# A hybrid attention and DeltaNet layer: the scan's small products grouped over both directions, the decay tile in two passes, softmax sums broadcast by transposes

## The chip, the cores and the metric

The kernel runs on one core of one Trainium2 chip. The metric is the device time of one execution in microseconds (us). Before the change three runs gave 896.90, 898.29 and 898.93 us; their median, 898.29 us, is the time to compare with.

## The reference, cut to what matters

One layer over 512 latent tokens and 256 context tokens, width 1024. A combined projection feeds two mixers: windowed attention with a softmax, and a gated DeltaNet that is scanned over chunks of 64 tokens, forwards and backwards, with 8 heads of 64. The scan's step, for each head and direction, is

```python
def step(S, xs):
    w_c, uv_c, qd_c, intra_c, kt_c, gl_c = xs
    u = uv_c - jnp.einsum('bhck,bhkv->bhcv', w_c, S)
    o = jnp.einsum('bhck,bhkv->bhcv', qd_c, S) + jnp.einsum('bhij,bhjv->bhiv', intra_c, u)
    S = jnp.exp(gl_c)[..., None, None] * S + jnp.einsum('bhck,bhcv->bhkv', kt_c, u)
    return S, o
```

The decays and rates of the scan come from 32 columns of the projection, `da` (through a softplus) and `db` (through a sigmoid). Attention outputs are divided by the softmax sums. After both mixers come their projections, gates, an output projection and a squared-ReLU MLP.

## The kernel before

**Engines and precision.** All data are float32. A projection is three TensorE matmuls per 128x128 block of weights (`mm3`, lines 312 to 314): both operands are split into a rounded high part and a low rest, and high times high, high times low and low times high are added up in one accumulator (in the profile `wh` and `wl` are the parts of a weight tile, `m` is any tile of the big arena). Other matmuls run on plain float32 and take two records each in the trace. PSUM's eight banks are handed out by `bank()`.

**Order of the work.** `tile_layer` records all instructions; then `arrange` lists them anew. `listed` walks through time with a table of costs: each engine takes the ready instruction that was recorded first, and TensorE stays with whole-array or with small-tile matmuls while the other kind is at most `STICK` = 50 instructions older. It also reckons with the arrival of TensorE's instructions, in blocks of 256 (`asked`). The order that results is fixed for each engine.

**The stages, in the order of the profile.**
- 0 to 60 us: modulation (`ada`, `columns`, `features`), with three early projection tiles. The first of these is `T_AB`: 32 useful columns (`da`, `db`) in a 128-wide block, the rest zeros. Its accumulator goes through lines 716 to 726 (a softplus and a sigmoid on 16 partitions each) into `gb`, which the small matmuls of line 753 read.
- To 280 us: key, query and value tiles, the matrices of the scan's chunks (`chunk_mats`), their inversion by a chain of pairs of VectorE operations (`invert`, lines 883 and 884), and attention (`scores`, `outputs`). Line 632 transposes the probabilities by `PE.transpose`; line 653 spreads a column of reciprocal softmax sums over 128 partitions by a plain float32 matmul with the identity, four for each of the eight (block, kv) units, and line 654 multiplies by them.
- 288 to 456 us: the scan, 4 context steps and 8 latent steps, each for two directions (`chain_step`), woven with filler matmuls (`br_a` at line 1105, `gate_tiles` at line 1059) and with `combine` (lines 904 to 915, 32x32 products).
- From 456 us: norm of the scan's output (line 1355, transposes at 1360), the branch and output projections and the MLP. `late_mod` (line 1124) is VectorE work that is spread over the scan and what follows.

**One scan step.** For a direction `d` and its state `S` a step has 64x64 products on TensorE: k times S and, for latent chunks, q times S (line 1175, 8 + 8 matmuls), then VectorE forms R (1179, 1180); XA times R gives u (1194, 8 matmuls); VectorE forms uk (1200), ScalarE copies u to `us` (1204) and, four times, the q product scaled to `zq` (1206); K times uk (1214, 8 matmuls) and VectorE's subtraction (1225) give the new state; IA times us (1232, 8 matmuls) and the additions of lines 1237 to 1242 give the output. All products of a direction lie in its own two banks, `zb[d]`. The 64x64 products are "small": TensorE goes from whole-array matmuls to them and back. A **visit** in this text is an uninterrupted run of small matmuls in TensorE's order.

## Time and profile before

| what | value |
|---|---|
| median of the three runs | 898.29 us |
| the profiled execution's own time | 895.83 us |
| its span in the profile | 894.1 us |
| mean granted TensorE clock | 0.998 |
| TensorE busy | 868.7 us of the span |
| VectorE, ScalarE busy | 652.3 us, 496.5 us |
| TensorE visits, counted in the order | 78, of which 45 in the latent scan |

PE is TensorE's matmul pipeline, PEld its weight loads, DVE VectorE, ACT ScalarE, SP the engine that issues most DMAs. A row of the timeline has the start in us, the duration in us, the engine, the line, the operation, `output<-input`, the shape and the number of records; `[0.63 <-PE ...]` is idle time before the row and what ended it. Matmuls overlap, so what one costs is the distance from its start to the next start.

### The profile page before, as it was taken

Reading aid. Unit: us, or ns where it says so; the run is one execution under the profiler, and the core shown is the slowest. Engines: PE = TensorE matmul, PEld = TensorE weight load, DVE = VectorE, ACT = ScalarE, POOL = GpSimd, SP = SyncE. Lnnn points to the kernel's source line nnn. Section 1 sums busy time; section 2 is a strip of 40 time slices with the busy share of each in tenths; the row PEclk is TensorE's granted clock in tenths of the full one; section 3 lists DMA queues with packets and bytes.
Section 4 is the critical chain, followed back from the end, with each engine's and each line's share of the span. In section 5 each row is a group of like instructions: output and inputs, shape, how many; then the busy total and the mean of one; then the engine's idle time right before and its main releaser. Section 6 shows DMA issues by size and latency. Waiting matters only on the chain.

```text
span 894.1 us, 18035 instructions
## 1 busy us (share of the span) xinstructions
PE 868.7 (97%) x7564; PEld 719.3 (80%) x7564; DVE 652.3 (73%) x1111; ACT 496.5 (56%) x881; POOL 26.1 (3%) x42
## 2 busy tenths in 40 slices
PE   7999999999999999999999999999999999999998
PEld 6778778877777777767678899888998899889886
DVE  5756899986778999856687878993868377638641
ACT  5549874486668886676654435561554245425520
POOL 0000001010000001100000000000000000000000
PEclk9999999999999999999999999999999999999999
DMA  9834455433111136623144653633314341332031
GB/s 354 325 101 95 91 129 124 108 78 66 36 36 32 64 115 244 211 73 97 49 154 154 226 175 118 209 121 128 108 48 138 98 137 52 118 114 100 1 118 47
DMA packets 31985, 107.13 MB, mean 120 GB/s; under 512 B 4000, under 2 KB 4512, under 8 KB 31904
## 3 DMA queue, kind: packets, MB, share of 16 engines
q1 hardware_dynamic: 29600, 97.59, 31.9%
q0 software_dynamic: 2304, 8.39, 5.7%
q8 instruction: 59, 0.97, 0.4%
q14 instruction: 22, 0.18, 0.1%
HBM read 103.87 MB, written 2.10 MB: 119 GB/s over the span
## 4 chain that ended last, share of the span: by engine, by line
PE 49%; DVE 3%; ACT 2%; DMA 1%; issue 1%; DVEq 0%; SPq 0%; ACTq 0%
PE banks L1528 12%; PE banks L313 10%; PE banks L314 10%; PE banks L312 10%; PE banks L1059 5%; DMA m<-in_wm 1%; DVE m L221 1%; PE banks L1175 1%; DVE m L318 1%; ACT m L220 1%; DVE m L320 1%; DMA m<-in_wada 0%; PE banks L1232 0%; PE banks L1214 0%; PE banks L1194 0%
## 5 line engine op out<-in xcount | busy, mean ns | idle before, releaser
L312 PE MATMUL banks<-m,wh 128*128 128x512 f32 (+1 forms) x568 | 213.0, 375 | 0.0
L313 PE MATMUL banks<-m,wh 128*128 128x512 f32 (+1 forms) x568 | 210.3, 370 | 0.6 <-DVE m L221 0.6
L314 PE MATMUL banks<-m,wl 128*128 128x512 f32 (+1 forms) x568 | 210.2, 370 | 0.0
L290 ACT ACTIVATE wh<-wr 128x1024 fp32r<-128x1024 f32 (+1 forms) x92 | 90.5, 984 | 135.5 <-PE banks L313 95.6
L1528 PE MATMUL banks<-m,m 128*128 128x256 f32 x1008 | 123.3, 284 | 3.6 <-ACT m L220 3.1
L1528 PEld LDWEIGHTS banks<-m,m 128*128 128x128 f32 x1008 | 122.0, 192 | 5.1 <-ACT m L220 3.7
L220 ACT ACTIVATE m<-m 128x512 fp32r<-128x512 f32 (+2 forms) x118 | 81.8, 719 | 75.3 <-PE banks L1528 16.0
L314 PEld LDWEIGHTS banks<-m,wl 128*128 128x128 f32 x568 | 106.9, 188 | 18.9 <-issue 0.7
L313 PEld LDWEIGHTS banks<-m,wh 128*128 128x128 f32 x568 | 107.0, 188 | 18.5 <-DVE m L221 1.1
L312 PEld LDWEIGHTS banks<-m,wh 128*128 128x128 f32 x568 | 107.1, 189 | 18.3 <-issue 0.5
L1059 PE MATMUL banks<-m,wh 128*128 128x512 f32 x320 | 108.0, 408 | 1.7 <-ACT m L181 0.8
L221 DVE TENSOR_TENSOR m<-m,m 128x512 fp32r<-128x512 f32 (+2 forms) x118 | 92.4, 805 | 21.4 <-ACT m L220 14.7
L295 DVE TENSOR_TENSOR wl<-wr,wh 128x1024 fp32r<-128x1024 f32 (+1 forms) x76 | 84.2, 1110 | 16.4 <-ACT wh L290 14.2
L1655 DVE SCALAR_TENSOR_TENSOR m<-banks,modT,m 128x512 f32<-128x512 f32 x32 | 24.0, 750 | 74.8 <-PE banks L314 74.7
L1059 PEld LDWEIGHTS banks<-m,wh 128*128 128x128 f32 x320 | 58.2, 188 | 14.5 <-ACT m L181 1.4
L1059 PE MATMUL banks<-m,wl 128*128 128x512 f32 x160 | 64.6, 404 | 0.6 <-DVE wl L295 0.6
L313 PE MATMUL banks<-m,m 128*128 128x256 f32 (+1 forms) x136 | 45.7, 342 | 0.5 <-DVE m L320 0.5
L312 PE MATMUL banks<-m,m 128*128 128x256 f32 (+1 forms) x136 | 45.0, 345 | 0.9 <-ACT m L319 0.8
L314 PE MATMUL banks<-m,m 128*128 128x256 f32 (+1 forms) x136 | 44.5, 336 | 0.2 <-DVE m L295 0.2
L1124 DVE SCALAR_TENSOR_TENSOR m<-m,m 128x1024 f32<-128x1024 f32 x32 | 38.7, 1219 | 5.0 <-DMA m<-in_wada 5.0
L1059 PEld LDWEIGHTS banks<-m,wl 128*128 128x128 f32 x160 | 30.0, 188 | 7.3 <-DVE wl L295 1.0
L181 ACT ACTIVATE m<-banks,st 128x512 f32<-128x512 f32 (+1 forms) x32 | 23.5, 738 | 20.3 <-DVE st L589 20.1
(258 smaller groups left out, 1345.4 us busy)
## 6 DMA issues: line engine op xcount, KB each, us to landing
m<-in_wada SPq DMA_DIRECT2D x48, 512.0 KB, 5.7
wr<-in_wm SPq DMA_DIRECT2D x40, 512.0 KB, 3.6
wr<-in_win SPq DMA_DIRECT2D x39, 512.0 KB, 3.5
m<-in_wm SPq DMA_DIRECT2D x24, 512.0 KB, 3.6
wl<-in_win POOLq DMA_DIRECT2D x16, 512.0 KB, 5.5
m<-in_xT SPq DMA_DIRECT2D x8, 512.0 KB, 5.5
wr<-in_wbr SPq DMA_DIRECT2D x16, 256.0 KB, 2.6
wr<-in_wout SPq DMA_DIRECT2D x8, 512.0 KB, 3.9
```

The costliest lines, as they stand in the source:

```text
L181: r = A.activation(out_, in_, func, **kw)
L220: A.activation(r32(hi), src, AF.Copy)
L221: (eng or V).tensor_tensor(r32(lo), src, hi, op=ALU.subtract)
L290: upper[0] = A.activation(r32(hi), raw, AF.Copy)
L295: V.tensor_tensor(r32(lo), raw, hi, op=ALU.subtract)
L312: PE.matmul(acc, w[0][:, k, :], xhi, start=(start and i == 0), stop=False)
L313: PE.matmul(acc, w[0][:, k, :], xlo, start=False, stop=False)
L314: r = PE.matmul(acc, w[1][:, k, :], xhi, start=False, stop=(stop and i == n - 1))
L1059: PE.matmul(acc.ap, w[x][:, k, :], hx[k][y], start=(k == p == 0), stop=(k == KT - 1 and p == 2))
L1124: V.scalar_tensor_tensor(wa.ap, wa.ap, 0.5, scr.ap, op0=ALU.mult, op1=ALU.mult, accum_out=modT[:, grp, j:j + 1])
L1528: PE.matmul(dst, r32(self.w[w][i][:, k * P:(k + 1) * P]), xs7[x][k][j], start=(n == 0), stop=(n == 11))
L1655: V.scalar_tensor_tensor(xn_[ct], accs[ct].ap, modT[:, 3, ct:ct + 1], xn_[ct], op0=ALU.mult, op1=ALU.add)
```

## The change

**The decay tile.** `T_AB` leaves the packed weights; its 64 columns come as an own array `wab`. Their high parts fill columns 0 to 63 of one 128-wide tile and their low parts columns 64 to 127 (`wload_ab`), so two matmuls per block instead of three give all products, and rows 64 to 127 of the accumulator are added to rows 0 to 63 afterwards: a ScalarE copy and a VectorE addition stand ahead of the softplus. The load is 256 KB instead of 512 KB.

**Softmax sums.** Line 653's matmul becomes `PE.transpose`, 32 in all.

**The scan.** The matmuls of a step are put in three lists for both directions (`runs`): list 0 k times S, list 1 XA times R, list 2 K times uk, q times S (moved here from list 0) and IA times us. `listed` holds all matmuls of such a list back until the last of them is ready and then releases them together. q times S and IA times us get two banks of their own, `qo`, shared by the directions; the scaled copies to `zq` come after list 2. From the start of the latent scan fillers have two banks instead of four.

**The planner's model of instruction arrival** has other constants. `LIMIT` is so large that its branch is never taken.

```diff
+    def wload_ab():
+        raw = wp.tile([P, KT, P], F32, tag="wr", bufs=NWR, name=nm("wr"))[:, :4].rearrange("p k (h c) -> p (k h) c", h=2)
+        nc.sync.dma_start(out=raw, in_=I["wab"])
+        b = alloc(1024)
+        ebufs.append(b)
+        w = b.ap.rearrange("p (k c) -> p k c", k=KT)
+        upper[0] = A.activation(r32(w[:, :, :CH]), raw, AF.Copy)
+        V.tensor_tensor(r32(w[:, :, CH:]), raw, w[:, :, :CH], op=ALU.subtract)
+        return r32(w), None
...
             PE.matmul(acc, w[0][:, k, :], xhi, start=(start and i == 0), stop=False)
-            PE.matmul(acc, w[0][:, k, :], xlo, start=False, stop=False)
-            r = PE.matmul(acc, w[1][:, k, :], xhi, start=False, stop=(stop and i == n - 1))
+            end = stop and i == n - 1
+            r = PE.matmul(acc, w[0][:, k, :], xlo, start=False, stop=(end and w[1] is None))
+            if w[1] is not None:
+                r = PE.matmul(acc, w[1][:, k, :], xhi, start=False, stop=end)
...
-            PE.matmul(rb[:, j * P:(j + 1) * P], st[:, 2, j:j + 1].broadcast_to([P, P]), ident, start=True, stop=True)
+            PE.transpose(rb[:, j * P:(j + 1) * P], st[:, 2, j:j + 1].broadcast_to([P, P]), ident)
...
-    V.tensor_scalar(ad, acc[0:16, :TOK], dtb[0:16], None, op0=ALU.add)
+    ab = t2[64:128]
+    A.activation(t2[0:64], acc[64:128, :TOK], AF.Copy)
+    V.tensor_tensor(ab, t2[0:64], acc[0:64, :TOK], op=ALU.add)
+    acc.free()
+    V.tensor_scalar(ad, ab[0:16], dtb[64:80], None, op0=ALU.add)
...
+        def small_product(n, out_, w, x):
+            runs[n].append(PE.matmul(out_, w, x, start=True, stop=True).ins.name)
...
         if S is not None:
-            for x, src in enumerate((kT, qT) if lat else (kT,)):
...
+            state_product(0, kT, zt)
...
             A.activation(by2(us.ap), u, AF.Copy)
-            for q in range(4):
-                A.activation(zq[:, UPOS[q] * HD:(UPOS[q] + 1) * HD], zt[:, ZP[q], 128 + 64 * (q % 2):192 + 64 * (q % 2)], AF.Copy,
-                             scale=eG[:, d, c * 4 + q:c * 4 + q + 1])
...
         if lat:
+            state_product(2, qT, two(0))
+            o2 = two(1)
...
             us.free()
+            yield
+            for q in range(4):
+                A.activation(zq[:, UPOS[q] * HD:(UPOS[q] + 1) * HD], two(0)[:, ZP[q], 64 * (q % 2):64 * (q % 2) + 64], AF.Copy,
+                             scale=eG[:, d, c * 4 + q:c * 4 + q + 1])
...
+    qo[0] = bank(2)
     ot_ = alloc(2048, True)
...
-def listed(steps, before, stick=STICK):
+def listed(steps, before, gangs):
...
+                if k in gang:
+                    g = gang[k]
+                    wait[id(g)] -= 1
+                    if not wait[id(g)]:
+                        go = max(ready[at[x]] for x in g)
+                        for x in g:
+                            heapq.heappush(coming["PE"], (go, at[x]))
...
-                block = int(words / 256 + .55)
-                if block > int(had / 256 + .55):
-                    asked[block] = t + 2350 + min(3000, max(0, links["SP"] - t - 1500))
-                t = max(t, asked.get(int(had / 256 - .6), 0))
+                block = int(words / 256 + .63)
+                if block > int(had / 256 + .63):
+                    asked[block] = max(t + 1100, links["SP"] - 500) + 1250
+                t = max(t, asked.get(int(had / 256 - .54), 0))
```

**What moves.** In the changed program the lines are counted anew: 1078 is the old 1059, 1194 any scan product, 923/924 and 933/934 the old 904/905 and 914/915, 693 the old 677, 741 the old 722.

TensorE in a latent step of before (lines 1194, 1214, 1232 are the scan's products, 1059 the filler):

```order
L1194 MATMUL banks<-m_4785,m_3495 64x64 x8
L1059 MATMUL banks<-m_152,wl_4519 128x512
L1059 MATMUL banks<-m_152,wh_4518 128x512
L1194 MATMUL banks<-m_4804,m_3499 64x64 x8
L1059 MATMUL banks<-m_152,wh_4518 128x512
L1059 MATMUL banks<-m_152,wl_4519 128x512
L1059 MATMUL banks<-m_152,wh_4518 128x512 x2
L1214 MATMUL banks<-m_4823,m_3384 64x64 x8
L1059 MATMUL banks<-m_152,wl_4519 128x512
L1059 MATMUL banks<-m_152,wh_4518 128x512 x2
L1232 MATMUL banks<-m_4825,m_3888 64x64 x8
L1214 MATMUL banks<-m_4840,m_3322 64x64 x8
```

The same place in the changed program, from list 1 of a step to the start of its list 2:

```order
L1078 MATMUL banks<-m_151,wh_4310 128x512 x2
L1194 MATMUL banks<-m_4612,m_3480 64x64 x8
L1194 MATMUL banks<-m_4623,m_3484 64x64 x8
L1078 MATMUL banks<-m_151,wl_4311 128x512
L1078 MATMUL banks<-m_151,wh_4310 128x512 x2
L1078 MATMUL banks<-m_151,wl_4311 128x512
L1078 MATMUL banks<-m_151,wh_4310 128x512 x2
L1078 MATMUL banks<-m_151,wl_4311 128x512
L1194 MATMUL banks<-m_4642,m_3307 64x64 x8
L1194 MATMUL banks<-m_2810,m_1889 64x64 x2
L1194 MATMUL banks<-m_2810,m_2380 64x64 x2
L1194 MATMUL banks<-m_2810,m_2226 64x64 x2
```

Both directions now stand next to each other, and list 2 is a run of 48. Over the whole program TensorE's order has 58 visits instead of 78: 24 instead of 45 in the latent scan and 9 instead of 8 at line 245. In one latent step lists 1 and 2 follow each other with no filler between them, a run of 64; the last list is followed by 43 fillers ahead of the first transposes of the scan's output, where before 27 stood.

TensorE in the second `combine` of before, between its first products (904, 905) and its second (914, 915), ten fillers:

```order
L905 MATMUL banks<-m_3500,m_795 32x32
L1059 MATMUL banks<-m_152,wh_3317 128x512 x2
L1059 MATMUL banks<-m_152,wl_3318 128x512
L1059 MATMUL banks<-m_152,wh_3317 128x512 x2
L1059 MATMUL banks<-m_152,wl_3318 128x512
L1059 MATMUL banks<-m_152,wh_3434 128x512 x2
L1059 MATMUL banks<-m_152,wl_3435 128x512
L1059 MATMUL banks<-m_152,wh_3434 128x512
L914 MATMUL banks<-m_3495,m_3537 32x32
```

And in the changed program, one filler:

```order
L923 MATMUL banks<-m_3481,m_781 32x32
L924 MATMUL banks<-m_3485,m_781 32x32
L1078 MATMUL banks<-m_151,wh_3419 128x512
L933 MATMUL banks<-m_3480,m_3522 32x32
L934 MATMUL banks<-m_3484,m_3522 32x32
```

101 small products stand ahead of that filler and 65 behind it; before, 63 stood ahead of the ten and 99 behind.

ScalarE where the decay tile is taken over, before:

```order
L319 ACTIVATE m_153<-m_508,modS 128x256
L677 ACTIVATE m_595<-banks,c_prm 128x512
L181 ACTIVATE m_581<-banks 16x768
L677 ACTIVATE m_595<-banks,c_prm 128x256
L181 ACTIVATE m_581<-m_581,onec 16x768
L722 ACTIVATE m_583<-m_583 16x768
```

And after the change (733 is the new copy):

```order
L335 ACTIVATE m_152<-m_493,modS 128x256
L733 ACTIVATE m_567<-banks 64x768
L693 ACTIVATE m_580<-banks,c_prm 128x512
L693 ACTIVATE m_580<-banks,c_prm 128x256
L693 ACTIVATE m_581<-banks,c_prm 128x512
L181 ACTIVATE m_564<-m_567 16x768
L693 ACTIVATE m_581<-banks,c_prm 128x256
L181 ACTIVATE m_564<-m_564,onec 16x768
L181 ACTIVATE m_564<-m_564 16x768
```

The sigmoid's first exponential moves behind the new copy and one more of the key tiles' copies. Behind the last transposes of the scan's output TensorE's order is the old one but for a few places.

## The prediction

> **What bounds the kernel now.** I read the page first, then busy time by stretches, then TensorE's rows in the latent scan.

> ```profile
> span 894.1 us, 18035 instructions
> PE 868.7 (97%) x7564; PEld 719.3 (80%) x7564; DVE 652.3 (73%) x1111; ACT 496.5 (56%) x881; POOL 26.1 (3%) x42
> ```
> ```profile
> 25.00:50.00 25.00, 24.68 (x176) 19.23 (x169) 17.56 (x37) 10.48 (x19) 0.74 (x1) 0.98 0.77 287
> 200.00:225.00 25.00, 23.00 (x145) 18.31 (x142) 17.63 (x32) 17.51 (x32) 0.86 (x1) 1.00 0.31 63
> 400.00:425.00 25.00, 24.95 (x479) 17.40 (x470) 17.10 (x39) 16.55 (x55) 0.00 (x0) 1.00 0.29 92
> 425.00:450.00 25.00, 25.00 (x521) 16.70 (x523) 17.49 (x42) 16.02 (x55) 0.00 (x0) 1.00 0.18 53
> ```

> In the second fence stand stretch, its length, busy time of PE, PEld, DVE, ACT and POOL, then the granted clock. TensorE is busy throughout, and VectorE and ScalarE have a third of their time free in the scan. So TensorE sets the end, and its time is what the change has to save. The clock is at its full value but for the start. But "busy" hides something:

> ```profile
> 424.94 0.69 PE L1175 MATMUL banks<-m,m 64*64 64x64 f32 x32
> 425.56 0.49 PE L1059 MATMUL banks<-m,wh 128*128 128x512 f32 x1
> ...
> 426.38 0.50 PE L1059 MATMUL banks<-m,wl 128*128 128x512 f32 x1
> 426.71 0.40 PE L1059 MATMUL banks<-m,wh 128*128 128x512 f32 x1
> 427.04 0.46 PE L1194 MATMUL banks<-m,m 64*64 64x64 f32 x16
> 427.43 0.50 PE L1059 MATMUL banks<-m,wh 128*128 128x512 f32 x1
> 427.77 0.39 PE L1059 MATMUL banks<-m,wl 128*128 128x512 f32 x1
> ```

> Distances between starts are the costs. 32 small records take 0.62 us up to the next filler and 16 take 0.39, so 16 more cost 0.23 to 0.28 and the leaving of a visit about 0.11 (0.39 - 0.28). A filler takes 0.23 elsewhere; the one ahead of the visit takes 0.33 (426.71 to 427.04), the first one behind it 0.34 (427.43 to 427.77). A visit costs 0.10 + 0.11 + 0.10 = 0.31 us over its products. The two bounds from neighbouring rows are 0.26 (a run with exit 0.06) and 0.34.

> **The change part by part.** All terms are against the profiled execution, 895.83 us (its span and 1.73 us around it). The median, 898.29, lies 2.46 above it; I subtract the gain from the median.

> *1. Decay tile, TensorE.* One pass of three goes for eight blocks, in the 512-wide and the 256-wide half.

> ```profile
> 44.50 0.39 PE L314 MATMUL banks<-m,m 128*128 128x512 f32 x1
> 44.73 0.28 PE L312 MATMUL banks<-m,m 128*128 128x256 f32 x1
> 44.84 0.28 PE L313 MATMUL banks<-m,m 128*128 128x256 f32 x1
> ```

> 8 x 0.23 + 8 x 0.11 = 2.7 us. One visit more at line 245 gives back 0.3: 2.4 us. The stretch 25 to 50 us was 24.68 of 25 busy, so nearly all of it should count; if the modulation chain became the limit there it would be nothing, so 0 to 2.7. The load halves, which can only help.

> *2. Decay tile, its way out.* A ScalarE copy and a VectorE addition of 64x768 come ahead of the softplus, and two more copies of the key tiles are queued ahead of the sigmoid's exponential.

> ```profile
> 59.95 1.00 DVE L716 TENSOR_SCALAR m<-banks,c_prm 16x768 f32<-16x768 f32 x1 [1.13 <-PE banks L314]
> 61.30 0.80 ACT L181 ACTIVATE m<-banks 16x768 f32<-16x768 f32 x1
> ...
> 69.76 0.60 DVE L726 TENSOR_SCALAR m<-m,nega 16x768 f32<-16x768 f32 x1
> ```
> ```profile
> 77.69 1.60 PE L753 MATMUL banks<-c_selq,m 64*64 64x40 f32 x48
> ```

> The operations are of the size of the first two rows: 1.0 + 0.8, and the two copies about 1.2. The old chain ended at 70.4 and its reader starts at 77.7: 7.3 us of cover, of which TensorE's earlier arrival takes 2.4. 7.3 - 2.4 - 3.0 leaves 1.9 us, so I put it at nothing. TensorE's matmuls of lines 312 to 314 are the cover; without it the cost would be up to 3 us. Queued behind the copy on ScalarE are the key tiles' convolution copies, which hold two banks each 0.8 us longer; they are as far ahead of their readers.

> *3. Softmax sums.* Four plain matmuls against four transposes:

> ```profile
> 206.60 0.60 PE L632 MATMUL banks<-c_ident,m 128*128 128x128 f32 x4
> 206.96 0.48 PE L314 MATMUL banks<-m,wl 128*128 128x512 f32 x1
> ...
> 208.41 1.06 PE L653 MATMUL banks<-c_ident,st 128*128 128x128 f32 x8
> 209.22 0.48 PE L621 MATMUL banks<-m,m 128*128 128x512 f32 x1
> ```

> Transposes: 0.36 for 4, 0.09 each. Line 653: 0.81 for 8 records, four matmuls, 0.20 each. 32 x 0.11 = 3.5 us of TensorE time. No row shows a transpose of a broadcast column, so the bounds are 0 (as dear as now) and 3.5. TensorE is only 23.0 of 25 busy here, where ScalarE and VectorE are waited for, so I count 0.8 of each microsecond: 2.8 us. [...]

> *4. Scan, visits.* The order has 21 visits less in the latent scan (24 for 45): 21 x 0.31 = 6.5 us, by the bounds 5.5 to 7.1. The number of products stays the same. Against that stand the groups' new waits, each worked out from one step.

> ```profile
> 427.58 0.42 DVE L1200 TENSOR_TENSOR m<-banks,eg 128x256 f32<-128x256 f32 x1 [0.63 <-PE banks L1194]
> ...
> 442.68 0.41 DVE L1242 TENSOR_REDUCE oss<-m 128x4 f32<-128x256 f32 x1
> 443.01 0.41 DVE L1179 TENSOR_TENSOR m<-banks,eg 128x256 f32<-128x256 f32 x1
> ```

> VectorE starts 0.54 after a group of eight does (427.04 to 427.58), and then takes 0.33 for each queued operation. Between lists 0 and 1 stand four operations (1179 and 1180 for both directions): 0.54 + 3 x 0.33 + 0.42 + 0.1 to tell TensorE = 2.05. TensorE's own work from list 0 to list 1 is 16 products (0.56), the visit's 0.31 and six to nine fillers at 0.23: 2.25 or more. Between lists 1 and 2 two operations take 0.54 + 0.33 + 0.42 + 0.1 = 1.4, and six fillers with list 1 give 2.25. Behind list 2 the second direction's state is ready 32 products on: 1.1 + 0.25 + 0.42 + 0.1 = 1.9, where list 2 itself (48 products, 1.7) and one filler with its visit give 2.2. So the groups wait for nothing, by margins of 0.2 to 0.8 us, but in one step: lists 1 and 2 stand there without fillers, 1.4 - 0.56 = **0.8 us lost**. Queued behind the groups are only fillers, and for those nobody waits in the scan. The old wait of line 1214 for the scaled copies in its own bank goes, since these now lie in `qo`: **1.2 us gained**.

> ```profile
> PE banks L915 <- issue: 2.8, 2, 2.1
> PE banks L1214 <- ACT m L1206: 1.2, 2, 1.0
> ```

> Two banks instead of four for fillers: a gate tile is 24 fillers, 5.5 us, and its evacuation two operations of under 1 us each, so the other bank is free in time; uncovered it would cost about 1 us for each of some five tiles.

> *5. Scan's end.* The last list is followed by 43 fillers, 43 x 0.23 + 1.1 + 0.2 = 11.2 us from its start to the transposes.

> ```profile
> 455.59 0.75 PE L1232 MATMUL banks<-m,m 64*64 64x64 f32 x32
> ...
> 458.68 1.22 DVE L1124 SCALAR_TENSOR_TENSOR m<-m,m 128x1024 f32<-128x1024 f32 x1
> ...
> 461.62 2.36 DVE L1355 TENSOR_TENSOR m<-m,oss 128x1024 f32<-128x1024 f32 x2
> ...
> 462.93 1.06 PE L1360 MATMUL banks<-c_ident,m 128*128 128x128 f32 x8
> ```

> VectorE has to finish more first than now, as its new order shows: five of line 1124's operations stand among the additions where two stood. From the list's start: 0.5 and four scaled copies (0.9) to the first addition, six operations at 0.33 (2.0), five at 1.22 (6.1), then 2.36: 11.9, and 0.1 to tell TensorE. **0.8 us lost**, between 0 and 2 since ScalarE could be late too.

> *6. Instruction delivery.* In the second `combine` ten fillers between two runs of small products become one.

> ```profile
> q8 instruction: 59, 0.97, 0.4%
> ```
> ```profile
> 344.08 0.21 PE L905 MATMUL banks<-m,m 32*32 32x32 f32 x1
> ...
> 348.65 0.19 PE L914 MATMUL banks<-m,m 32*32 32x32 f32 x1
> 350.98 0.21 PE L915 MATMUL banks<-m,m 32*32 32x32 f32 x1 [2.13 <-issue]
> ...
> 351.99 0.50 PE L1059 MATMUL banks<-m,wh 128*128 128x512 f32 x1
> ```

> 59 packets for 2 x 7564 records of matmuls and loads is about 256 records a packet, and a small product takes four. 162 products and ten fillers, 668 records, took 7.9 us here, 2.13 of it with nothing to wait for but the issue. If delivery sets the pace, the new stretch (166 products, one filler, 666 records) also takes 7.9 us and holds nine fillers less: 2.1 us lost. If not, nothing, or even 2.1 gained where the stall doesn't come. I take one more stall of the mean size of the two on record (2.8 / 2): **1.4 us lost**. [...]

> The sum: 2.4 + 2.8 + (6.5 + 1.2 - 0.8 - 0.8) - 1.4 = **9.9 us**. 895.8 becomes 885.9 in the profile, and the median 898.3 becomes **888.4**.

> **The rivals.**
> - *The early gains hide.* Terms 1 and 3 turn into waits for VectorE and ScalarE. For it: TensorE is idle for 2.0 of 25 us in the attention stretch shown; against it: that is 92% busy. What is left is 6.1 - 1.4 = 4.7: **893.6**.
> - *The transposes aren't cheaper.* A single record is long (0.60 for four at 0.09 apart leaves 0.33), and only the distance between starts is short. Without term 3: **891.2**.
> - *Delivery and the scan's end cost their upper bounds* (2.1 and 2.0): **890.3**. The other way, with no more stall, it would be 887.0. [...]
> - *The groups make the recurrence the bound, slower than before.* Both directions now wait for the later of the two, three times a step. The place is list 1, behind four VectorE operations, or more where output additions or a weight's rest (1.2 us) stand between. My margin there is 0.2 us. Against it: VectorE is idle for 30% of the scan. The price is the mean wait of the 24 groups: it turns the sign at 9.9 / 24 = 0.41 us a group. With 0.6 it would be 24 x 0.6 - 9.9 = 4.5 us slower, **902.8**.

> **How the numbers follow.** My forecast, 886 to 891, 0.52; early gains hidden 0.15; transposes not cheaper 0.07; upper bounds of terms 5 and 6 0.10; recurrence bound 0.13, of which 0.10 is slower and 0.03 about even; better than 886 0.03. A measurement of this kernel tells 0.2%, 1.8 us, from no change; another 0.03 of the hidden case falls within that. Faster 0.84, same 0.06, slower 0.10. The range reaches from all terms at their best but for the stalls (885) to the hidden case with its own waits (895).

> **What would show it.** Right: the third pass's 16 matmuls gone before 60 us at no new wait at the old line 753; rows of line 669 at 0.09 apart; 24 visits in the latent scan with gaps under 0.3 us but for one; an issue stall in the second `combine` of over 2 us; a wait of about 0.8 us ahead of the transposes after the scan. Wrong: TensorE idle ahead of most groups, with VectorE as what ended it, or a larger share of waits between 180 and 280 us.

## The result, and the profile after

Five runs of the changed kernel gave 902.70 to 906.95 us, median **905.32**; five of the kernel before 896.90 to 899.33, median 898.85. The ratio is 1.0078 (95% interval 1.0059 to 1.0096): **0.8% slower**, where 888.4 us and a gain were forecast. The profiled execution took 905.58 us, 9.75 us more than that of before. Single executions of one kernel lie up to 11 us apart (e8 and e11 below); a likely reason will be seen below. In what follows, "before" without a time is the kernel before. The line numbers of experiments lie up to four off those of the kernels they come from, and in e11 to e14, which have parts of the change alone, up to 19 off those of before.

The page, first its head and then the busy time by stretches (columns as in the prediction):

```profile
span 903.8 us, 17921 instructions
PE 863.5 (96%) x7516; PEld 717.1 (79%) x7516; DVE 651.9 (72%) x1112; ACT 495.7 (55%) x882; POOL 26.1 (3%) x42
```
```profile
25.00:50.00 25.00, 24.48 (x177) 17.99 (x177) 18.34 (x39) 12.82 (x24) 0.00 (x0) 1.00 0.73 280
200.00:225.00 25.00, 21.83 (x125) 17.17 (x124) 16.72 (x31) 15.13 (x27) 0.86 (x1) 0.93 0.23 48
275.00:300.00 25.00, 21.22 (x122) 15.86 (x120) 23.06 (x42) 22.25 (x43) 0.00 (x0) 0.93 0.11 32
350.00:375.00 25.00, 19.56 (x415) 15.56 (x416) 17.37 (x28) 11.52 (x23) 4.15 (x8) 0.80 0.76 265
400.00:425.00 25.00, 25.00 (x546) 19.13 (x545) 18.26 (x40) 18.27 (x62) 0.00 (x0) 1.00 0.36 114
425.00:450.00 25.00, 23.15 (x578) 17.63 (x580) 18.78 (x47) 17.42 (x63) 0.00 (x0) 1.00 0.18 59
```

TensorE is 5.2 us less busy, as a change that takes work away should make it, and yet the span is longer: it stands idle more. And the granted clock, 1.00 in the prediction's rows from 200 us on, is now 0.93 in two of these stretches and 0.80 in a third. The idle time by what ended it, from TensorE's waits:

```profile
PE banks L1124 <- ACT m L966: 3.2, 1, 3.2
PE banks L923 <- issue: 2.9, 1, 2.9
PE banks L934 <- issue: 2.6, 2, 1.5
PE banks L1078 <- ACT m L181: 2.2, 1, 2.2
PE banks L597 <- ACT m L181: 2.0, 1, 2.0
PE banks L1194 <- ACT m L1233: 1.5, 1, 1.5
PE banks L326 <- ACT wh L290: 1.1, 1, 1.1
```

Put side by side, the starts of the same instructions tell where the time went. By each place the two kernels have done different numbers of fillers (0.23 us each), and the right column takes these out: at the second `combine`'s start the changed kernel has done 8 more fillers than before, at its end none more, at the transposes 15 more.

| place | before | after | lost in the stage, fillers taken out |
|---|---|---|---|
| first small products of the old line 753 | 77.69 | 75.46 | -2.2 |
| end of the first `combine` | 196.29 | 193.62 | -0.4 |
| start of the second `combine` | 341.40 | 344.70 | +4.1 |
| its last 32x32 product | 362.34 | 369.98 | +6.2 |
| transposes after the scan (old line 1360) | 462.93 | 470.22 | -3.8 |
| end of TensorE's work | 890.24 | 899.99 | +5.9 |

So the decay tile gained about what was said, the scan 3.8 of the 6.1 us, and three other stages lost 16 us. All this is from one execution of each kernel.

**What half a clock has to do with it.** The second `combine` in stretches of 3.41 us:

```profile
345.49:348.90 3.41, 3.41 (x58) 2.59 (x58) 3.41 (x5) 2.86 (x4) 0.00 (x0) 1.00 0.31 112
348.90:352.31 3.41, 1.05 (x123) 0.94 (x111) 3.41 (x6) 2.98 (x8) 0.00 (x0) 0.99 0.86 300
352.31:355.72 3.41, 2.81 (x128) 2.17 (x128) 3.20 (x6) 0.00 (x0) 0.00 (x0) 0.50 0.99 365
355.72:359.13 3.41, 2.04 (x61) 1.81 (x62) 2.75 (x5) 0.94 (x2) 0.92 (x2) 0.50 1.00 376
362.55:365.96 3.41, 3.41 (x29) 2.56 (x30) 0.35 (x1) 1.66 (x2) 0.00 (x0) 1.00 0.56 168
```

TensorE is busy for 1.05 of 3.41 us, and for the next three stretches its clock is 0.50. It does not come back at once: in the 17 traces of this study, from 45 us on, it came back behind each of the 47 halved stretches in which TensorE was busy for 0.87 or more, and stayed halved behind each of the 13 with 0.27 to 0.86, as here behind 2.81 and 2.04 of 3.41 us. In the profiles of before and of the changed kernel the clock changes only at multiples of 3.41 us from one another (what lies between two changes lasts 3.41, 10.24, 17.07 or 20.48 us, or longer); in the changed kernel's it is 0.50 for 27 us ((1 - 0.985) x 2 x 903.8), in before's for some 4 ((1 - 0.998) x 2 x 894.1). I divided all 17 traces into such stretches, from 45 us on, and took those at full clock. Ahead of 45 us the table doesn't hold: there the clock also fell behind a stretch with TensorE busy for 2.33 of 3.41 us (68%, from 19.27 us on in before), so that the time of TensorE's records can't be all that counts.

| TensorE busy in a stretch of 3.41 us | stretches | followed by a stretch at half clock |
|---|---|---|
| under 0.45 | 41 | 39 |
| 0.45 to 0.55 | 17 | 8 |
| 0.55 and more | 3888 | 0 |

Five of the 41 are the changed kernel's, from 209, 287, 349, 380 and 837 us on, each with a stretch at half clock behind it; before has none under 0.55.

What an idle time cost therefore depended on where it fell. The same wait of the MLP, in before and in an experiment told below (e13, latent groups alone):

```profile
828.30:831.70 3.40, 1.85 (x16) 1.65 (x14) 1.98 (x4) 2.86 (x5) 0.00 (x0) 1.00 0.00 0
831.70:835.10 3.40, 2.96 (x24) 2.96 (x25) 2.53 (x3) 1.49 (x3) 0.00 (x0) 1.00 0.00 0
```
```profile
831.50:834.90 3.40, 1.42 (x12) 1.22 (x11) 3.17 (x4) 1.70 (x3) 0.00 (x0) 0.99 0.00 0
834.90:838.30 3.40, 3.40 (x18) 3.40 (x18) 1.87 (x3) 1.15 (x2) 0.00 (x0) 0.50 0.00 0
838.30:841.70 3.40, 3.40 (x30) 3.40 (x30) 3.04 (x6) 0.60 (x1) 0.00 (x0) 1.00 0.00 0
```

In before the wait of 1.99 us is split between two stretches (1.85 and 2.96 busy), and nothing follows. In the other it falls into one (1.42 of 3.40), and the next stretch does 18 records in the time of 30, which costs 12/30 of 3.4 = 1.4 us. The phase of the stretches is not the same in two traces (the clock falls at 22.68 us in before and at 21.18 us in the changed kernel, 1.50 us apart), and if it also differs between executions of one kernel, these can differ by it; that is an inference. Their mean clocks fit it: of e11's twelve executions the one at 0.999 took 892.56 us and the one at 0.986 took 903.48 us.

(Some expectations below place the half-clock stretches at 208, 287, 348 and 379 us: they count 4.1 us less than the profile, where these start at 212, 291, 352 and 383.)

### The profile page after: what moved, and what is told of

Its sections match the earlier page's. It is cut to its first block, busy times and chain, and to the rows that moved or that the text cites. A ratio compares the mean times of both kernels' runs of the same rounds, so it can differ in the third digit from the quotient of the medians.

```text
span 903.8 us, 17921 instructions
## 1 busy us (share of the span) xinstructions
PE 863.5 (96%) x7516; PEld 717.1 (79%) x7516; DVE 651.9 (72%) x1112; ACT 495.7 (55%) x882; POOL 26.1 (3%) x42
## 4 chain that ended last, share of the span: by engine, by line
PE 78%; ACT 9%; DVE 7%; DMA 3%; issue 2%; SPq 0%; DVEq 0%; ACTq 0%
PE banks L326 14%; PE banks L328 13%; PE banks L330 13%; PE banks L1565 12%; PE banks L1078 11%; PE banks L1194 3%; PE banks L1124 2%; ACT m L181 2%; PE banks L648 1%; ACT m L220 1%; DVE m L221 1%; DMA m<-in_wm 1%; PE banks L711 1%; DVE m L334 1%; PE banks L638 1%
## 5 line engine op out<-in xcount | busy, mean ns | idle before, releaser
L326 PE MATMUL banks<-m,m 128*128 128x256 f32 (+1 forms) x136 | 45.8, 350 | 0.4 <-ACT m L335 0.3
L328 PE MATMUL banks<-m,m 128*128 128x256 f32 (+1 forms) x136 | 44.9, 342 | 0.3 <-DVE m L336 0.3
L330 PE MATMUL banks<-m,m 128*128 128x512 f32 (+1 forms) x120 | 39.5, 334 | 0.1
L1194 PEld LDWEIGHTS banks<-m,m 64*64 64x64 f32 x1600 | 26.8, 134 | 13.9 <-issue 4.3
```

The source lines that it names most:

```text
L326: PE.matmul(acc, w[0][:, k, :], xhi, start=(start and i == 0), stop=False)
L328: r = PE.matmul(acc, w[0][:, k, :], xlo, start=False, stop=(end and w[1] is None))
L330: r = PE.matmul(acc, w[1][:, k, :], xhi, start=False, stop=end)
L1194: runs[n].append(PE.matmul(out_, w, x, start=True, stop=True).ins.name)
```

## The experiments

Ratios are to the kernel before on the same chip.

| run | median, us | ratio (95% interval) |
|---|---|---|
| changed kernel | 905.32 | 1.0078 (1.0059 to 1.0096) |
| e1 ungrouped | 906.85 | 1.0116 (1.0097 to 1.0135) |
| e2 matmul sums | 908.07 | 1.0122 (1.0105 to 1.0138) |
| e3 fillers in all bursts | 912.58 | 1.0175 (1.0154 to 1.0197) |
| e4 transposes alone | 902.81 | 1.0063 (1.0049 to 1.0078) |
| e5 transposes, padded | 902.24 | 1.0051 (1.0036 to 1.0066) |
| e6 shorter warm-up | 903.64 | 1.0063 (1.0041 to 1.0085) |
| e7 changed, padded | 913.14 | 1.0173 (1.0143 to 1.0202) |
| e8 fillers in combine | 899.15 | 1.0020 (1.0000 to 1.0040) |
| e9 unaware planner | 903.56 | 1.0064 (1.0043 to 1.0085) |
| e10 all mended | 898.77 | 1.0004 (0.9987 to 1.0022) |
| e11 decay tile alone | 896.77 | 0.9995 (0.9974 to 1.0016) |
| e12 groups alone | 899.25 | 1.0015 (1.0002 to 1.0028) |
| e13 latent groups alone | 896.80 | 0.9981 (0.9967 to 0.9996) |
| e14 latent groups, fillers | 903.31 | 1.0059 (1.0038 to 1.0080) |
| e15 addition on GpSimd | 899.41 | 1.0014 (0.9997 to 1.0030) |

### Where the instructions' blocks end: e4, e6, e5, e7

**e4**, before with transposes, its order kept:

```diff
-            PE.matmul(rb[:, j * P:(j + 1) * P], st[:, 2, j:j + 1].broadcast_to([P, P]), ident, start=True, stop=True)
+            AS_M.add(PE.transpose(rb[:, j * P:(j + 1) * P], st[:, 2, j:j + 1].broadcast_to([P, P]), ident).ins.name)
...
-                return (110, 280) if self.ins.is_transpose else (max(62, 1.72 * n), max(62, 1.72 * n) + 170)
+                return (110, 280) if self.ins.is_transpose and self.name not in AS_M else (max(62, 1.72 * n), max(62, 1.72 * n) + 170)
...
-                one = s.dtype.endswith("32r") or s.dtype.endswith("16") or s.ins.is_transpose
+                one = s.dtype.endswith("32r") or s.dtype.endswith("16") or (s.ins.is_transpose and s.name not in AS_M)
```

> The kernel before with transposes for the 32 broadcasts and nothing else; the planner counts them as matmuls, so the order is that of before, instruction for instruction. If a transpose saves 0.11 us and four fifths of it count: 898.9 - 2.8 = 896.0 (895.4 at most). If it is hidden by waits in the attention stretch: 898.9. If transposes are idle time for the clock's gate: a half-clock window more in the attention stretch, 898 to 900.

It got 0.6% slower, 5.9 us by the medians, with nothing changed but 32 instructions that became cheaper. Against before's trace, instruction by instruction, each group of four takes 0.46 us less, but all groups' gains but one are taken back by the waits for VectorE and ScalarE that follow: at 281 us the lead is 0.46 us, not 2.8. No half-clock stretch comes in the attention. Then the second `combine`:

```profile
348.16 0.21 PE L916 MATMUL banks<-m,m 32*32 32x32 f32 x1 [0.54 <-issue]
...
354.08 0.26 PE L906 MATMUL banks<-m,m 32*32 32x32 f32 x1 [4.64 <-issue]
...
367.98 0.18 PE L916 MATMUL banks<-m,m 32*32 32x32 f32 x1 [1.40 <-issue]
```

Before had 2.13 and 0.71 us here. The 32 transposes have two records each in the place of four, 64 less. **e6** takes away 64 records that have nothing to do with transposes:

```diff
-    for _ in range(NONES):
-        PE.matmul(wb_[:, :P], ones, ones, start=True, stop=True)
+    for _ in range(14):
+        EXTRA[PE.matmul(wb_[:, :256], ones, ones.unsqueeze(1).broadcast_to([P, 2, P]), start=True, stop=True).ins.name] = 120 / 14
```

> The kernel before, where 14 warm-up matmuls of 256 columns stand for the 30 of 128: 64 TensorE records less at the start, and nothing else; the order is that of before. Theory 1 (where a block of 256 records ends decides): the stall of the second combine grows from 2.1 to about 4.6 us, that of the next from 0.7 to 1.4, and two half-clock windows (6.8 us at half speed) follow: 896.9 + 5.5 to 6 = about 902.6, as with the transposes alone. Rival (a matter of the transposes): 896.9, as before.

```profile
353.78 0.26 PE L906 MATMUL banks<-m,m 32*32 32x32 f32 x1 [4.91 <-issue]
...
366.29 0.18 PE L916 MATMUL banks<-m,m 32*32 32x32 f32 x1 [0.55 <-issue]
```

The same loss of 0.6%, without a transpose. Counting TensorE's records (matmuls, weight loads and the few semaphore records among them) from the start of each trace, the issue waits stand at

```
before   6082, 6593        e4  5826, 6082, 6593     e6  5826, 6082, 6593
e5       3522, 6082        e13  6082, 6593          changed kernel  5826, 6082, 6593, 7361
```

All 40 issue waits of 0.35 us or more in the 17 traces, from 45 us on, stand at a multiple of 256 plus 193 or 194, whatever instruction falls there. I read this as instructions that come in blocks of 256 records, each ending at such a position; the page of before fits it, with 59 instruction packets for 2 x 7564 records (256 each), but no row shows the delivery itself. A small product takes four records, so that a block holds 64 of them, little more than 1 us of work (in the changed kernel the stretch from 348.90 us on has 123 of their matmul records, two a product, in 1.05 us). In e4 and e6 the burst of 99 products begins 0.06 of a block ahead of an end and runs over the next too; in before it begins 0.19 behind one and runs over one only. From the second `combine`'s start to its last product e4 took 6.3 us more than before, of which 3.7 are the longer issue waits; two half-clock stretches behind the long wait fit the rest.

**e5** adds 16 tiny warm-up matmuls to e4 and cuts the width of the other 30 from 128 to 96 columns, which puts the blocks back:

```diff
+    for _ in range(16):
+        EXTRA[PE.matmul(wb_[:, :8], ones, ones[:, :8], start=True, stop=True).ins.name] = 0
```

> The kernel before with the transposes, as in the run with the transposes alone, and 16 tiny matmuls more (8 columns) among the warm-up matmuls at the start, whose own width is cut to 96 columns; the order of all else is that of before. The 16 matmuls are 64 TensorE records, as many as the transposes took away, so that record 6082 falls again on the same product of the second combine as in before. Theory 1 (TensorE's instructions come in blocks of 256, and what the transposes changed is only where in the burst of small products a block ends): the stalls are those of before (2.1 and 0.7 us), no half-clock window follows, and the time is that of before less the half microsecond that the transposes save: 896.4. Rival (the transposes themselves cost it, by their effect on the clock or on the order of arrival in the attention stretch): 902.8 as without the tiny matmuls.

In the second `combine` it did what was expected: one wait of 1.74 us, no half clock, 1.3 us less than before for that stretch where e4 took 6.3 more. The median missed, since the tiny matmuls weren't free (the 16 took 3.6 us, and the old line 753 comes 3.3 us later), and a block now ends at record 3522, right behind the first `combine`:

```profile
201.73 0.44 PE L585 MATMUL banks<-m,m 128*128 128x384 f32 x1 [1.85 <-issue]
```

**e7** does the same to the changed kernel, with `range(28)`.

> The changed kernel with 28 tiny matmuls (112 records) among the warm-up ones, the order else being its own. The second combine's burst then lies at records 22.06 to 24.65 in units of 256 instead of 21.62 to 24.21, its blocks end at 22.76 and 23.76 as ever, so that the first end comes 0.7 of a block after the burst's start, fetched long before. Theory 1: the stall of 2.9 us at 22.76 goes, that at 23.76 may grow to 2 us, that at 25.75 goes or halves, and two or three half-clock windows go: 905.3 - 3 - 4 = about 898, 896 to 901. Rival (the stretch takes as long whatever the position of the blocks): 905.

It missed by 15 us, and in large part for the same reason: the 28 tiny matmuls took 9.1 us, and the start got 9.5 us slower (old line 753 at 84.95 for 75.46). The waits at 5826 and 6593 went as expected, that at 6082 grew to 3.08 us, and the stretch from the first long burst to the last product took 17.3 us in the place of 21.5.

### Filling the bursts: e8, e3

**e8** lets the planner take fillers between `combine`'s products when it reckons that the next block is late:

```diff
-LIMIT = 1e9
+LIMIT = 2
...
-            if not steps[k].whole and asked.get(block, 0) - t > LIMIT * ((block + .54) * 256 - words):
+            if not steps[k].whole and steps[k].tile == (HC, HC) and asked.get(block, 0) - t > LIMIT * ((block + .54) * 256 - words):
```

> The changed kernel with LIMIT at 2, but for the 32x32 products of combine alone; the scan's groups stay whole (60 visits in all, against 58 in the changed kernel and 70 with the limit everywhere). Theory 1 (late instructions and the half-clock windows behind them cost some 9 us in the second combines): the stalls of 5.5 us and the three windows at 348 us go, two visits more cost 0.6, some fillers miss later in the scan (up to 2 us): 905.3 - 5.5 - 4 + 0.6 + 1 = about 897.5. Rival (fillers moved out of the scan are missed there, and the recurrence is the bound): 903 to 912, as with the limit everywhere.

The issue waits of `combine`'s products sink from 5.5 us to 0.3, no half clock follows there, and three quarters of the loss are gone (1.0020 for 1.0078). In its trace the stage of the second `combine` is 1.2 us shorter than in before (fillers taken out), where the changed kernel's was 6.2 longer. This is the largest single cause that an edit could take away. **e3** is the same without the test for the tile.

> The changed kernel with LIMIT at 2 in the place of 1e9: where the planner reckons that instructions arrive late, it takes whole-array fillers between small products, so that the second combine's bursts of 101 and 65 products are cut by 9 to 16 fillers. Theory 1 (late instructions leave TensorE idle for 5.5 us in the two second combines, and three or four half-clock windows follow, 13.7 us at half speed): stalls and windows go, 5.5 + about 5 us gained, 12 visits more cost 3.7 us: about 898.5. Rival (instructions arrive at a fixed rate and the stretch takes as long whatever stands in it): stalls move elsewhere, 905 to 909.

No issue wait was left in the second `combine` either, and yet it was the slowest but one. The scan's groups were cut apart (70 visits), and what the rival of the prediction feared came there:

```profile
PE banks L1078 <- ACT m L181: 4.0, 1, 4.0
...
PE banks L1194 <- ACT m L1233: 3.1, 2, 2.0
...
PE banks L1194 <- DVE m L1208: 1.7, 3, 1.3
```

### What the planner made of cheaper transposes: e2, e9

**e2** puts matmuls back in the changed kernel and keeps its order (wherever the planner asks for `is_transpose`, the names in `AS_T` count too):

```diff
-            PE.transpose(rb[:, j * P:(j + 1) * P], st[:, 2, j:j + 1].broadcast_to([P, P]), ident)
+            AS_T.add(PE.matmul(rb[:, j * P:(j + 1) * P], st[:, 2, j:j + 1].broadcast_to([P, P]), ident, start=True, stop=True).ins.name)
```

> The changed kernel with plain float32 matmuls for the 32 broadcasts of line 669; the planner still counts them as transposes, so the order is that of the changed kernel, instruction for instruction. Theory 1 (a transpose is 0.11 us cheaper): 905.3 + 2.8 = 908.1, at most 908.8. Rival A (no cheaper in this place, since TensorE waits for VectorE and ScalarE there): 905.3 within 1. Rival B (transposes don't count as work for the clock's gate, so they bring the half-clock window at 208 us): that window goes and the time falls by up to 1.7 us, to about 904 to 906.

2.8 us by the medians, as theory 1 had it; but by e4 the transposes save 0.5 us, and the trace puts the difference elsewhere. The second `combine`'s stage is 3.8 us shorter than in the changed kernel, since the records shift by 64 (one issue wait of 3.77 us, one half-clock stretch for three). From the first `combine` to the second it is 5.8 us longer, with the same idle time (9.5 us for 9.8) but four half-clock stretches for two, and the start is 1.9 us later. So this run doesn't tell what the transposes are worth. The half-clock stretch at 217 us stays, so the transposes don't bring it.

ScalarE at that place, in the changed kernel:

```profile
207.34 1.06 ACT L290 ACTIVATE wh<-wr 128x1024 fp32r<-128x1024 f32 x1 [1.24 <-PE banks L328]
...
209.74 1.06 ACT L292 ACTIVATE wl<-wh 128x1024 fp32r<-128x1024 f32 x1 [0.82 <-ACT m L220]
210.70 0.78 ACT L181 ACTIVATE m<-banks,st 128x640 f32<-128x640 f32 x1
```
```profile
211.62 0.44 PE L597 MATMUL banks<-m,m 128*128 128x384 f32 x1 [1.97 <-ACT m L181]
```

Two weight splits stand ahead of the softmax exponential, for which TensorE waits 1.97 us; in before they stand behind it. They moved because the planner books a transpose at 110 ns for 220. **e9** is the changed kernel with the planner counting them as matmuls (the edits of `AS_M` in e4).

> The changed kernel, all of its parts, but the planner counts the 32 broadcasts as matmuls as it did before (220 ns and four records in place of 110 ns and two). Its order then keeps ScalarE's softmax exponential ahead of the weight splits of lines 290 and 292 in the attention stretch, as before's does. Theory 1 (the wait of 1.97 us at 211 us comes from the order that the planner makes of cheaper transposes, and a half-clock window follows it): both go, 905.3 - 2 - 1.7 = about 901.5, if the second combine's stalls stay as they are (its bursts are now 63, 4 fillers, 101). Rival (that wait comes from the decay tile or the groups): 905.

The wait and its half-clock stretch are gone, 0.28 us is left, and the wait at 290 us is 1.58 us for 3.24, with no half-clock stretch behind it. The gain by the ratios is 0.14% (1.0064 for 1.0078), 1.3 us and not 3.7: the blocks end elsewhere again, and the issue waits of `combine` are 8.5 us (3.3, 2.9, 2.3).

### The groups: e1, e12, e13, e14

**e1** empties the list of groups in the changed kernel:

```diff
-    return ties, gangs
+    return ties, []
```

> The changed kernel, but the products of the scan's lists are no longer held back for one another (the list of groups handed to the planner is empty). Theory 1 (the loss is idle stretches that the new order puts into TensorE's work, each made dearer by a half-clock window behind it): the wait of 3.2 us at the scan's start (line 1124 behind line 966) goes, since list 1 of the first direction can run there again, with the half-clock window behind it (1.7 us), and so does the wait of 2.2 us at 383 us with its window; five visits more cost 1.6 us, the stalls of the second combine stay: 905.3 - 4.9 - 3.9 + 1.6 = about 898. Theory 2 (the groups save what was forecast and everything is lost elsewhere, above all in the second combine): 905.3 + 1.6 = about 907.

The wait at 290 us sank from 3.24 to 1.35 us, that at 383 us stayed (2.26), and the whole got slower: theory 2 was nearer. Yet from the second `combine` to the transposes its trace gains 4.0 us against before, as much as the changed kernel. The order has 63 visits, only five more than with the groups, since the two directions' lists are recorded next to each other either way. So 16 of the 21 visits saved come from the lists and their own banks, and holding products back saves the five others; that no half-clock stretch follows the wait at 383 us in this trace may hide some of it.

**e12** has the scan's part alone, on before.

> The kernel before with the scan's lists, groups and own banks and the new arrival constants, but without the decay tile's two passes and without the transposes. By the forecast the latent scan gains 6.1 us. Theory 1 (the groups also hold back the first context step's products, 3.2 us of idle time with a half-clock window behind it, and a wait of about 2 us comes at 382 us): 898 - 6.1 + 4.9 + 2 = about 899, 897 to 903 with the second combine's stalls. Rival (the recurrence became the bound): no gain in the latent scan at all, 905.

899.25, as expected. **e13** is e12 without groups in the four context steps:

```diff
-            gangs.extend(runs)
+            gangs.extend(runs if step >= NCC else [])
```

> The kernel before with the groups (and their own banks) in the latent steps alone; context steps are not grouped, decay tile and broadcasts as before. The second combine's bursts are those of before (63, 10 fillers, 99, 28 fillers), on the same records. Theory 1 (the groups' saving of about 6 us is real in the scan and is given back in part behind it, at the weights of 490 to 500 us): stalls as in before, 3 to 4 us ahead of before where the norm's transposes start (after allowance for 15 fillers more that are done by then), about 0 to 3 us faster at the end: 895 to 898. Rival (the waits for groups and filler banks eat it in the scan): 898 to 901.

This is the best version of all: 0.9981, **0.19% faster than before** (0.04 to 0.33%), and 0.34% better than e12. Context groups hold back products that TensorE could do at 290 us while it waits for ScalarE (1.6 us idle there in e12 and e9, 3.2 in the changed kernel, none over 0.8 in e13). What lists, banks and latent groups are worth together: from the second `combine`'s last product to the transposes e13 takes as long as before (100.5 against 100.6 us) with 15 fillers more done, 3.5 us. Two waits are new in it, at 377 us (2.26 us, with a half-clock stretch) and 433 us (1.48). Behind the transposes its profile, which is of the slowest of its twelve executions, gives more than that back (6.3 us, with the half-clock stretch in the MLP that was shown above):

```profile
PE banks L313 <- ACT wh L291: 2.5, 2, 1.4
```

This row is the weights of the branch and output projections, which stood ready in before and now come 2.5 us late.

**e14** is e13 with e8's edits.

> As the run with the latent groups alone, and combine's products cut by fillers (LIMIT at 2 for 32x32 products). If late instructions still cost 2.8 us there: 2 us faster than the latent groups alone, 893 to 896. If fillers taken from the scan are missed there: the same or up to 2 us slower.

It came out 7 us above the range of the first case, and 4.5 above the second: the `combine` stage got 2.9 us shorter than in e13 (fillers taken out), but fillers that went into it were missing in the scan. From there to the transposes it took 6.3 us longer than e13, and a block's end met the products of the old line 805 (2.35 us of issue).

### All together: e10, e11, e15

**e10** joins e8's, e9's and e13's edits in the changed kernel.

> The changed kernel with three edits: the planner counts the broadcasts as matmuls, combine's products are cut by fillers (LIMIT at 2 for 32x32 products alone), and only the latent steps' products are grouped, not those of the four context steps. Theory 1 (the change's own savings are real, and the loss is the idle stretches at 211 us, 290 us and in the second combine with the half-clock windows behind them): 905.3 - 3.7 - 2.5 to 4.9 - 6 + 1.6 for five visits more = 893 to 895, faster than before by 0.3 to 0.6%. Rival (something that all versions with the groups share, such as the wait at 382 us or the weights at 502 us, eats the savings): 898 to 900.

It comes out even with before (1.0004). At the transposes it is 3.4 us ahead with 15 fillers more done, 6.8 us in all; at the end of TensorE's work 0.3. Waits of 1.1 and 0.7 us for the weights at 492 us, with a half-clock stretch behind them, and some 1.6 us more of idle time in the MLP took most of it. The trace is of the fastest of its twelve executions, with no half clock at the start.

**e11** is the decay tile alone.

> The kernel before with the decay tile in two passes and nothing else; the planner orders freely. Theory 1: 2.4 us gained ahead of 60 us, and the stream is some 30 records shorter, so that the second combine's last block end lies 0.1 of a block later in its burst; with that stall as in before 896.9 - 2.4 = 894.5, with stalls like those of the transposes alone about 900. Rival (the gain is hidden by the start's loads): 897.

No difference (0.9995). In its profile the first part is not faster at all (old line 753 at 77.77 us), while the changed kernel and e10 gained 2.2 and 3.2 us there. The clock between 15 and 40 us, in e11 and in e10:

```profile
15.00:40.00 25.00, 22.83 (x156) 15.47 (x154) 16.75 (x35) 12.86 (x23) 0.00 (x0) 0.80 1.01 407
```
```profile
15.00:40.00 25.00, 21.75 (x171) 14.49 (x170) 19.14 (x38) 13.72 (x26) 0.00 (x0) 1.00 1.01 405
```

This stretch waits for loads (the DMA column, last but one, is full), TensorE's work in it has gaps, and how long the clock is halved there differs from trace to trace. Ahead of 45 us it is halved for 3.4 us in each of the five traces without the decay tile and with the old warm-up (before, e4, e12, e13, e14), and for 0 to 13.7 us in the nine with it, 7.6 in the mean. The gain at the old line 753 goes with it: 3.2 us with none (e10), 2.2 with 3.4 (the changed kernel), 1.8 and 2.3 with 6.8 (e9, e8), -0.1 to 0.4 with 10.2 (e2, e11, e15), -1.3 with 13.7 (e1); only e3, whose order differs at the start, loses 1.6 with 6.8. That 4.2 us more of half clock cost about 2.1 us, all that the tile saves, is an estimate from one execution of each kernel.

**e15** moves one of VectorE's four operations of each branch tile in e10 to GpSimd:

```diff
-        V.tensor_tensor(g, g, gat[ct].ap, op=ALU.add)
+        G.tensor_tensor(g, g, gat[ct].ap, op=ALU.add)
```

> The version with all three mends (e10), with line 1424's addition of the branch projections on GpSimd in the place of VectorE (eight operations of 128x512). Theory (VectorE's four operations per tile are the bound between 470 and 500 us): the waits of 1.1 and 0.7 us at 492 us and the half-clock window behind them go, 898.8 - 3.5 = about 895.3. Rival (the weights' own arrival is the bound, or GpSimd's addition is slow enough to be waited for): 898 to 902.

No gain: the waits at 496 us are as in e10 (1.10 and 0.78), though no half-clock stretch follows them in this trace. GpSimd's addition takes 1.55 us for VectorE's 0.69, and ScalarE's queue, in which the weight split stands, waits for it (for up to 2.95 us between 484 and 500 us):

```profile
L1424 POOL TENSOR_TENSOR m<-m,m 128x512 f32<-128x512 f32 x8 | 12.4, 1545 | 97.2 <-issue 86.8 <-DVE m L1422 8.3 <-ACT wh L291 2.1
```

So it doesn't tell whether VectorE is the bound there; that stays open.

## Why the prediction was wrong, point by point

**Step 6, instruction delivery, is the step that failed, and not it alone.** Between the gain of 9.9 us that was forecast and the 9.75 us lost lie 19.7 us. In the traces 6.5 of them lie ahead of the second `combine` (step 3), 4.8 in it (step 6), 2.3 in the scan (steps 4 and 5), 5.9 behind it, for which the prediction had no term, and 0.2 at the start. What the places share is that a wait was priced at its length and the clock taken as full: from 45 us on the clock is halved for seven stretches, which were in no term.

Of delivery the prediction said "I take one more stall of the mean size of the two on record (2.8 / 2): 1.4 us lost", and its upper bound was 2.1. The stage lost 6.2 us, and filling the bursts (e8) brought back 0.58%, 5.2 us. The reckoning went by how many records a stretch has, where the position of the blocks' ends in the burst decides (e4, e6): the waits are now

```profile
352.81 0.26 PE L923 MATMUL banks<-m,m 32*32 32x32 f32 x1 [2.86 <-issue]
...
357.09 0.26 PE L934 MATMUL banks<-m,m 32*32 32x32 f32 x1 [1.47 <-issue]
...
369.89 0.18 PE L934 MATMUL banks<-m,m 32*32 32x32 f32 x1 [1.16 <-issue]
```

5.5 us for 2.84. The rest of the 6.2 us, 3.5, fits the three half-clock stretches behind the first wait. "The clock is at its full value but for the start" was read as a property of the chip, where it was one of this order of work.

**Step 1, the decay tile: right in size**, 2.2 us for 2.4 at the old line 753, but as e11 shows the clock at the start can take it away; that the profiled execution had only 3.4 us of half clock there is luck. **Step 2: right**; the products of the old line 753 follow without a wait:

```profile
75.46 1.60 PE L772 MATMUL banks<-c_selq,m 64*64 64x40 f32 x48
```

**Step 3, the sums: price right, worth wrong.** Transposes stand 0.09 us apart (205.57 to 205.93 for four):

```profile
205.57 0.60 PE L669 MATMUL banks<-c_ident,st 128*128 128x128 f32 x4
205.93 0.47 PE L637 MATMUL banks<-m,m 128*128 128x512 f32 x1
```

But of 3.5 us not four fifths, only 0.5 counted (e4). "92% busy" said nothing on whether the next wait was tied to TensorE or to VectorE. The rival "the early gains hide" was right on this, and too kind: through the planner's costs the transposes also brought the wait of 1.97 us.

**Step 4, the scan: the mechanism (fewer visits) right, the size too large.** 6.1 us were forecast with step 5; 3.8 came in the changed kernel, 3.5 in e13. The groups don't wait for VectorE: the recurrence rival is out, all their waits in the latent scan are one of 1.5 us (for ScalarE's copy of line 1233) and one of 0.4. What was mis-sized is the price of two filler banks, "about 1 us" where uncovered. At 383 us ScalarE has 2.3 us of copies queued ahead of the evacuation for which the next filler waits, and a half-clock stretch follows:

```profile
379.99 1.06 ACT L290 ACTIVATE wh<-wr 128x1024 fp32r<-128x1024 f32 x1 [5.38 <-PE banks L1078]
381.07 1.28 ACT L1357 ACTIVATE m<-m 32x512 f32<-32x512 f32 x2
382.37 0.60 ACT L181 ACTIVATE m<-banks 128x512 f32<-128x512 f32 x1
```
```profile
383.02 1.22 PE L1078 MATMUL banks<-m,wh 128*128 128x512 f32 x2 [2.21 <-ACT m L181]
```

The first row shows that ScalarE itself had stood idle for 5.38 us, since a weight split stood first in its order and waited for TensorE's fillers; the copies behind it did not run in that time. In e8, with the same two banks, that split stands behind the evacuation, and no filler waits there; so the order on ScalarE counts, and not the number of banks alone, which was not tried by itself. Not foreseen at all was the first context step, where TensorE is idle for 3.24 us. The groups are only a part of it: 1.35 us is left without them (e1) and 1.58 with them in the order of e9.

**Step 5, the scan's end: wrong.** No wait came ahead of the transposes. The 0.91 us that stand earlier, ahead of a filler whose weight's rest is late, are another wait, and that they are near the 0.8 forecast is luck. What the scan saved is then lost again behind it (5.9 us in the last stage, of which some 1.7 are a half-clock stretch at 840 us, and the rest waits for weights and for the MLP's copies). The prediction stopped its account at the transposes.

Of the rivals none was it. The sign came in the main from idle times of 2 to 3 us in four places (212, 290, 353 and 383 us) with a half-clock stretch behind each. With all four cut short (e10: 0.3 to 1.0 us each) the loss is gone, though no gain is left. Two of them could have been looked for in the changed order: ScalarE's at 208 us, and the first context step's.

## What to carry to other kernels

Price an idle time of TensorE not by its length alone but by where it falls. Here the clock was halved behind 39 of the 41 stretches of 3.41 us, from 45 us on, in which TensorE was busy for less than 0.45, and a halved stretch cost 1.4 us more in e13 (18 records in the time of 30; half of 3.41, 1.7 us, is my estimate of the most). The 1.99 us that before waited in two stretches (1.85 and 2.96 of 3.40 us busy) brought no half clock, so split over two stretches the same wait was cheaper than in one. And the clock can stay low: behind the wait of 2.86 us in the changed kernel it stayed at 0.50 for three stretches, the first two busy for 2.81 and 2.04 us.

When a long burst of small matmuls is in a program, see where the issue waits fall in it before reading any small difference: here 64 records less, far ahead of the burst, moved them (2.13 us at the longest in before, 4.64 in e4, 4.91 in e6) and the time by 0.6%. Whole-array work in the burst took the waits away here (5.5 us in the changed kernel, 0.3 in e8), but it must come from where it is not missed: it gained 5.2 us in e8 and lost 6.5 in e14 against e13. And when a planner is told of a new cost, read its order everywhere, not only at the changed lines.
